# Gate and up projections of the SwiGLU turned round: activation forms as the held operand, 512 weight columns streaming

## The chip, the cores and the metric

The kernel runs on one core of a Trainium2 chip. The metric is the device time of one execution in microseconds (us). The kernel before has a median of 2325.04 us over three runs (2324.38 to 2325.2). The profiled execution shown here took 2325.69 us, of which 2323.9 us is the span from the first instruction to the last.

The engines are called as in the profile: PE is the matrix engine, PEld its weight loads, DVE the vector engine, ACT the scalar engine, POOL the general one and SP the queue that issues most transfers. In a matmul one operand, 128 columns wide, is held in the array (the "weights" of PE) and the other streams past it; the number of streaming columns is the last number of the shape in a row (128x256, 128x512).

## The reference

One layer of a hybrid encoder on 512 tokens with 2048 channels, in float32:

```python
h = rms_norm(x, norm1_g)
p = h @ w_in                      # columns for three mixers
y = concat(rwkv7, rglru, retention)
x = x + y @ w_out
h = rms_norm(x, norm2_g)
x = x + (silu(h @ ffn_w_gate) * (h @ ffn_w_up)) @ ffn_w_down
return rms_norm(x, final_norm_g)
```

The feed-forward width is 5632. The change touches the line with `ffn_w_gate` and `ffn_w_up` (two 2048 x 5632 matrices) and what lies directly beside it.

## The kernel before

Every float32 matmul is done as three: both operands are cut into a high part (rounded to the short format by a cast on ACT) and a low part (the remainder, a subtraction on DVE), and high·high, high·low and low·high are added up in one PSUM bank. `split` makes the two parts of a weight tile, `mm3` issues the three matmuls (lines 161 to 163 of the profile).

The gate and up projections are done with Strassen's scheme (Winograd's variant): the two matrices, each in two halves of channels, are the blocks b11, b21 (gate) and b12, b22 (up); the activations in two halves of channels and two halves of tokens give seven forms f = 0 to 6. Seven products of 1024 channels replace eight. Sums of weight blocks are DVE additions over [128, 1024], sums of results are DVE operations on PSUM banks.

The stages around it, in the order of the program:

1. `w_out`: the output projection. For each of 16 channel tiles PE adds up 16 channel blocks; then x1 = x + that is stored, squared into `acc`, scaled by `norm2_g`, and when both halves are there `make_forms` writes the seven forms, high and low. Five of eight form groups (NFA = 5) have tiles of their own (FAH, FAL); three lie in HH and HL, which hold `w_out`'s own operand, so those wait until that is consumed (the list `late`).
2. `gate_up(ct)` for 44 tiles of 128 feed-forward columns. The weight tile [128 channels, 128 columns] is held, the form [128 channels, 256 tokens] streams. A split weight piece is [128, 1024] and carries all eight channel blocks of one product; there are five places for split pieces (`fslot`, NFS = 5) and ten for raw ones. Results are feature-major: columns on partitions, tokens along the free dimension. The norm factor per token (`rB`, copied over all partitions) multiplies the gate result; ACT computes tanh, DVE two more operations, and the tile, with the up part not yet scaled by the norm, is stored to `hscr[ct]` in DRAM.
3. `down(ci, n)` for ten chunks of four feed-forward tiles, and `down_last` for the eleventh. `load_h` brings the tiles of the next chunk from `hscr`, multiplies by `rB` (the norm factor of the up part) and splits them into GH and GLo.

A scheduler sets the order in which each engine's instructions stand, once, when the program is built; work under `tc.high_priority()` is put ahead of other work that is ready. On the chip each engine then runs its list strictly in that order. Tiles live in pools; when `fa.close()` ends the pool of the gate/up stage, the tiles of the down stage (GH, FT, X1, RW2, ...) take over its memory and wait for its last readers.

Of the kernel before, what the change touches and what calls it, by code (L numbers as in the profile page):

```python
# [30 lines left out]
NFA = 5  # L31
# [7 lines left out]
for _n, _c in PAR:  # L39
# [4 lines left out]
CST = [("ident", 128), ("bd1", 128), ("mask", 128), ("maskr", 128),  # L44
       ("zero", 64), ("mD", 1), ("bd2", 2), ("invf", 1), ("sgn", 1), ("qec", 1), ("hec", 1),
# [6 lines left out]
NCST = _o  # L52

# [43 lines left out]
def hybrid_block(ctx: ExitStack, tc: tile.TileContext, A: dict, out: bass.AP, dbg=None):  # L97
# [32 lines left out]
    def c(name):  # L130
        o, n = CO[name]
        return cst[:, o:o + n]
# [49 lines left out]
    rB = cp.tile([128, T], F32, name="rB")  # L182
# [61 lines left out]
    with tc.high_priority():  # L244
        G.memset(zn, 0.0)
        act(zn[:, 0:1], zn[:, 0:1], AF.Tanh)
        nc.sync.dma_start(out=par, in_=A["par"])
        G.dma_start(out=cst, in_=A["cst"])
# [647 lines left out]

    fa = ExitStack()
    ap_ = fa.enter_context(tc.tile_pool(name="fa", bufs=1))
    RB = [ap_.tile([128, 2048], F32, name=f"RB{i}") for i in range(4)]
    FAH = ap_.tile([128, NFA, 7, 256], F32R, name="FAH")  # L900
    FAL = ap_.tile([128, NFA, 7, 256], F32R, name="FAL")
    XW = ap_.tile([128, 2, 1024], F32R, name="XW")
    EV = ap_.tile([128, 2, 3, 256], F32, name="EV")
    GT = ap_.tile([128, 2, T], F32, name="GT")
    UT = ap_.tile([128, 2, T], F32, name="UT")
    acc = rB
# [31 lines left out]
    def make_forms(j, F):  # L938
# [3 lines left out]
        tt(q[:, 7, :], q[:, 2, :], q[:, 6, :], SUB)  # L942
        hi, lo = form(0, j), form(1, j)
        for d, s_ in ((slice(0, 1), slice(0, 1)), (slice(1, 7), slice(2, 8))):
            S.copy(out=hi[:, d, :], in_=q[:, s_, :])
            tt(lo[:, d, :], q[:, s_, :], hi[:, d, :].bitcast(F32), SUB)

    ring.update(raw2=0, rawl=0, last=0, w2=0, gu=0, ft=0, dn=0, wo=0, rb=0, fs=0, ev=0, h=0)
    ob = {}
    late = []  # L950
    sq = UT
    for n, (ct, q) in enumerate(O_PIECES):
        if n % 2 == 0:
            pcs = wpieces1(A["w_out"][n // 2])
        if q == 0:
            xi = GT[:, nxt("h", 2), :]
# [6 lines left out]
        if q == 3:  # L963
# [9 lines left out]
            F = RB[j % 4]  # L973
            act(F[:, 512 * (ct // 8):512 * (ct // 8) + 512], x1, AF.Copy, scale=p("g2", ct))
            if ct >= 8:
                if j < NFA:
                    make_forms(j, F)
                else:
                    late.append((j, F))
    for j, F in late:  # L980
        make_forms(j, F)

    S.copy(out=rB, in_=head_rsqrt(acc, c("mD"), 1, mmb, eps=NORM_EPS))


    ring["rb"] = 8

    def gate_up(ct):
        b11, b21, b12, b22, x = (rslot(nxt("rb", 10)) for _ in range(5))
        with tc.high_priority():  # L990
            for t_, m, half in ((b11, 0, 0), (b21, 0, 1), (b12, 1, 0), (b22, 1, 1)):
                nc.sync.dma_start(out=t_, in_=A["w_gu"][ct, m, half])
        ps = [bank[nxt("gu", 8)] for _ in range(5)]

        def product(raw, f, b, first):
            wh, wl = fslot(nxt("fs", NFS))
            with tc.high_priority():
                split(raw, wh, wl)
            o = ps[b][:, 0:256]
            for j in range(8):  # L1000
                cs = slice(128 * j, 128 * j + 128)
                mm3(o, wh[:, cs], wl[:, cs], form(0, j)[:, f, :], form(1, j)[:, f, :], first and j == 0, j == 7, skip_group_check=not first)

        e = nxt("ev", 2)
# [327 lines left out]
```

## Time and profile before

| What | Value |
|---|---|
| Median of three runs | 2325.04 us |
| Profiled execution | 2325.69 us |
| Its span | 2323.9 us |
| PE busy | 2283.9 us (98%) |
| PEld busy | 2037.9 us (88%) |
| DVE busy | 1696.6 us (73%) |
| ACT busy | 988.6 us (43%) |
| POOL busy | 21.6 us (1%) |
| Granted PE clock over the span | 0.992 of full speed |
| Moved by DMA | 272.99 MB, mean 117 GB/s |

Matmuls overlap in the array, so the duration in a row (283 ns for 256 columns) is longer than the distance between the starts of two neighbours. What a matmul costs in a dense run is that distance. Granted clock 1.00 is 2.4 GHz and 0.50 is 1.2 GHz; the profile shows no other level, and a number between is a mean over a stretch.

The stages on the clock of the span: mixers up to 760 us, `w_out` to 922.7 us, gate and up to 1816.8 us, down and the last norm to the end.

### The profile page before, as it was taken

How to read it: one execution, taken by the hardware profiler on the slowest of the kernel's cores; microseconds unless marked ns; L12 is line 12 of the kernel's file. 1: busy time of each engine (PE TensorE's matmuls, PEld its weight loads, DVE VectorE, ACT ScalarE, POOL GpSimd, SP SyncE). 2: the span in 40 equal slices, each digit the busy share in tenths (PEclk: the TensorE clock that was granted, in tenths of full speed). 3: DMA queues.
4: the chain of work that ended last, by engine and by line, in shares of the span. 5: the costliest groups of instructions: out<-in, count | busy, mean ns of one | idle time of the engine just before them, and what ended most of it. 6: DMA issues, size and time to landing. Idle time of an engine off the chain costs nothing.

```text
span 2323.9 us, 36949 instructions
## 1 busy us (share of the span) xinstructions
PE 2283.9 (98%) x14529; PEld 2037.9 (88%) x14529; DVE 1696.6 (73%) x2925; ACT 988.6 (43%) x1650; POOL 21.6 (1%) x58
## 2 busy tenths in 40 slices
PE   8999999999999999999999999999999999999998
PEld 7878777778888887999999999999999788878887
DVE  7788699687656555888888888888888466576555
ACT  5563464454235444444444444444444432232234
POOL 0000000000000000000000000000000000000000
PEclk9999999999999999999999999999999999999999
DMA  5324233323323444344333343444332554454332
GB/s 199 102 80 112 75 98 93 107 82 108 106 64 106 153 158 148 131 123 123 117 111 115 118 123 114 123 123 122 111 114 91 159 151 135 132 150 128 117 105 73
DMA packets 131757, 272.99 MB, mean 117 GB/s; under 512 B 37296, under 2 KB 43696, under 8 KB 131456
## 3 DMA queue, kind: packets, MB, share of 16 engines
q1 hardware_dynamic: 120880, 250.47, 36.1%
q10 hardware_dynamic: 8448, 12.59, 1.4%
q0 software_dynamic: 2256, 7.58, 1.0%
q8 instruction: 114, 1.87, 0.3%
q14 instruction: 59, 0.48, 0.1%
HBM read 241.36 MB, written 27.66 MB: 116 GB/s over the span
## 4 chain that ended last, share of the span: by engine, by line
PE 91%; DVE 6%; ACT 1%; issue 1%; DMA 1%; DVEq 0%; SPq 0%; ACTq 0%
PE bank L161 28%; PE bank L162 28%; PE bank L163 28%; PE bank L166 5%; DVE M L140 1%; DVE WL L140 1%; PE bank L569 1%; PE bank L592 1%; DVE M L149 0%; DMA FT<-hscr 0%; DVE M L404 0%; DVE X L140 0%; DVE M L406 0%; DVE SM L140 0%; PE bank L493 0%
## 5 line engine op out<-in xcount | busy, mean ns | idle before, releaser
L161 PE MATMUL bank<-HH,WH 128*128 128x512 f32 (+1 forms) x1297 | 474.6, 366 | 9.1 <-ACT HH L152 6.2
L163 PE MATMUL bank<-HH,WL 128*128 128x512 f32 (+1 forms) x1297 | 472.4, 364 | 0.0
L162 PE MATMUL bank<-HL,WH 128*128 128x512 f32 (+1 forms) x1297 | 472.0, 364 | 0.0
L157 ACT CAST WH<-RAW 128x512 fp32r<-128x512 f32 (+1 forms) x356 | 236.1, 664 | 466.4 <-PE bank L162 403.2
L140 DVE TENSOR_TENSOR WL<-RAW,WH 128x512 fp32r<-128x512 f32 (+1 forms) x356 | 263.4, 740 | 139.8 <-ACT WH L157 137.9
L161 PEld LDWEIGHTS bank<-HH,WH 128*128 128x128 f32 x1297 | 246.1, 190 | 46.5 <-ACT HH L152 6.2
L163 PEld LDWEIGHTS bank<-HH,WL 128*128 128x128 f32 x1297 | 245.9, 190 | 36.3 <-issue 1.4
L162 PEld LDWEIGHTS bank<-HL,WH 128*128 128x128 f32 x1297 | 246.2, 190 | 35.6 <-issue 1.4
L161 PE MATMUL bank<-GH,WH 128*128 128x512 f32 x640 | 250.5, 392 | 6.6 <-ACT WH L157 4.3
L163 PE MATMUL bank<-GH,WL 128*128 128x512 f32 x640 | 250.4, 392 | 0.0
L162 PE MATMUL bank<-GLo,WH 128*128 128x512 f32 x640 | 250.4, 392 | 0.0
L140 DVE TENSOR_TENSOR X<-X,bank 128x512 f32<-128x512 f32 (+1 forms) x178 | 115.6, 655 | 143.0 <-PE bank L163 141.9
L163 PE MATMUL bank<-FAH,WL 128*128 128x256 f32 x615 | 174.8, 284 | 3.0 <-DVE WL L140 3.0
L161 PE MATMUL bank<-FAH,WH 128*128 128x256 f32 x615 | 174.9, 284 | 0.2 <-ACT WH L157 0.2
L162 PE MATMUL bank<-FAL,WH 128*128 128x256 f32 x615 | 174.6, 284 | 0.0
L162 PE MATMUL bank<-FAL,HH 128*128 128x256 f32 x615 | 174.0, 283 | 0.0
L163 PE MATMUL bank<-FAH,HL 128*128 128x256 f32 x615 | 174.0, 283 | 0.0
L161 PE MATMUL bank<-FAH,HH 128*128 128x256 f32 x615 | 173.9, 283 | 0.0
L161 PEld LDWEIGHTS bank<-GH,WH 128*128 128x128 f32 x640 | 121.2, 189 | 32.9 <-ACT WH L157 4.7
L157 ACT CAST HH<-RB 128x1024 fp32r<-128x1024 f32 x90 | 94.4, 1049 | 129.2 <-PE bank L162 79.6
L157 ACT CAST WH<-RB 128x1024 fp32r<-128x1024 f32 x87 | 91.4, 1050 | 126.9 <-PE bank L162 80.2
L163 PEld LDWEIGHTS bank<-GH,WL 128*128 128x128 f32 x640 | 121.1, 189 | 26.1 <-DVE WL L140 0.6
(255 smaller groups left out, 4980.5 us busy)
## 6 DMA issues: line engine op xcount, KB each, us to landing
RB<-in_w_gu_dram SPq DMA_DIRECT2D x132, 512.0 KB, 3.8
RAW<-in_w_in_dram SPq DMA_DIRECT2D x76, 512.0 KB, 3.5
RAW<-in_w_dn_dram SPq DMA_DIRECT2D x96, 256.0 KB, 2.7
RAW<-in_w_gu_dram SPq DMA_DIRECT2D x44, 512.0 KB, 3.7
RW<-in_w_dn_dram SPq DMA_DIRECT2D x80, 256.0 KB, 2.7
RAW<-in_w_out_dram SPq DMA_DIRECT2D x32, 512.0 KB, 3.5
hscr<-UT ACTq DMA_DIRECT2D x44, 256.0 KB, 4.2
FT<-hscr SPq DMA_DIRECT2D x40, 256.0 KB, 3.5
```

The lines of the kernel that those rows point to most:

```text
L140: (eng or V).tensor_tensor(out=o, in0=a, in1=b, op=op)
L157: S.copy(out=hi, in_=raw)
L161: PE.matmul(o, wh, xh, start=first, stop=False, **kw)
L162: PE.matmul(o, wh, xl, start=False, stop=False, **kw)
L163: PE.matmul(o, wl, xh, start=False, stop=last, **kw)
L166: PE.matmul(o, l, r, start=start, stop=stop)
L569: PE.matmul(F[:, q, hv[e]], LS[e][:, ch, :], VS[:, ch, hv[e]], start=(q == 0 and e == 0), stop=True, skip_group_check=(q > 0 or e > 0))
L592: PE.matmul(F[:, q, :], P_[q][1][:, ch, :], ZBq[:, q, :], start=False, stop=True, skip_group_check=True)
```

## The change

- The roles are exchanged in gate and up. A form [128 channels, 128 tokens] is held, and 512 weight columns stream. The stage runs over 11 blocks (NU) of 512 feed-forward columns, each with seven products on two token tiles of 128. One product is four pieces of [128, 1024] (two channel blocks by 512 columns), each used by twelve matmuls.
- Results are token-major, one PSUM bank for each token tile: bA, bB, bC are three pairs of banks, each used by two or three of the seven products. The norm factor is now one number per partition (`rh`, `r2h`), used as the scale of ACT's tanh and as the scalar of a DVE operation; both gate and up get it here, so `load_h` no longer multiplies by `rB`.
- The down stage still wants feature-major tiles, so each block ends with 16 transposes of [128, 128] on PE into two banks (6 and 7), four copies on ACT and four stores.
- Sums of weight blocks are now made once for 512 columns, over [128, 2048].
- Raw blocks: eight tiles of [128, 2048], one for each half block, no second copy. Split pieces: three places instead of five, since NFA is 4, four form groups now lie in HH and HL, and memory is taken by E, H, X2, G1. The late forms are written form by form (the order in which products ask for them) instead of group by group.
- Small things: `cst` is brought in two parts, three tiles move to the mixers' pool, RW2 is allocated earlier in the down pool, and the first chunk's `hscr` tiles go through FT instead of RAW.

The core of the diff:

```diff
-    def rslot(i):
-        return RB[i // 2][:, 1024 * (i % 2):1024 * (i % 2) + 1024] if i < 8 else RAW[:, i - 8, :]
-    NFS = 5
+        if i < 2:
+            return tuple(w[:, 2 * i:2 * i + 2, :].rearrange("p a b -> p (a b)") for w in (WH, WL))
+        return tuple(w.rearrange("p k t -> p (k t)")[:, 7168:8192] for w in (HH, HL))
...
+    for d, s_ in ((0, 0), (1, 2), (4, 5), (3, 4), (5, 6), (2, 3), (6, 7)):
+        for j, F in late:
+            form_put(j, F, slice(d, d + 1), slice(s_, s_ + 1))
-    S.copy(out=rB, in_=head_rsqrt(acc, c("mD"), 1, mmb, eps=NORM_EPS))
+    rq = head_rsqrt_stat(acc, c("mD"), 1, mmb, eps=NORM_EPS)
+    rh, r2h = drv[:, 0:4], drv[:, 4:8]
...
+    blocks = ((RB[0], RB[1]), (RB[4], RB[5]), (RB[2], RB[3]), (RB[6], RAWb))
...
-            wh, wl = fslot(nxt("fs", NFS))
-            with tc.high_priority():
-                split(raw, wh, wl)
-            o = ps[b][:, 0:256]
-            for j in range(8):
-                cs = slice(128 * j, 128 * j + 128)
-                mm3(o, wh[:, cs], wl[:, cs], form(0, j)[:, f, :], form(1, j)[:, f, :], ...)
+            for jj in range(4):
+                wh, wl = fslot(nxt("fs", 3))
+                with tc.high_priority():
+                    split(raw[jj // 2][:, 1024 * (jj % 2):1024 * (jj % 2) + 1024], wh, wl)
+                for t in range(2):
+                    tk = slice(128 * t, 128 * t + 128)
+                    for i in range(2):
+                        j, cs = 2 * jj + i, slice(512 * i, 512 * i + 512)
+                        mm3(bs[t], form(0, j)[:, f, tk], form(1, j)[:, f, tk], wh[:, cs], wl[:, cs], ...)
...
+        product(b11, 0, bA, True)
+        with hp_():
+            for t in two:
+                S.copy(out=E_[:, t, :], in_=bA[t])
+        block(b11, b11, b12)
+        product(b21, 1, bA, False)
+        with hp_():
+            for t in two:
+                act(G_[:, t, :], bA[t], AF.Tanh, scale=rh[:, t:t + 1])
+                stt(G_[:, t, :], G_[:, t, :], 1.0, bA[t], ADD, MUL)
+        block(b12, b12, b22)
+        product(b12, 4, bB, True)
+        product(b11, 3, bC, True)
+        block(b11, b11, b22)
+        product(b11, 5, bA, True)
+        with hp_():
+            for t in two:
+                tt(E_[:, t, :], bA[t], E_[:, t, :], SUB)
+                tt(H_[:, t, :], bB[t], E_[:, t, :], ADD)
+                tt(X_[:, t, :], bC[t], H_[:, t, :], ADD)
+        block(b21, b21, b11)
+        product(b21, 2, bB, True)
+        with hp_():
+            for t in two:
+                tt(H_[:, t, :], bB[t], H_[:, t, :], SUB)
+                act(bB[t], H_[:, t, :], AF.Tanh, scale=rh[:, 2 + t:3 + t])
+                stt(H_[:, t, :], bB[t], 1.0, H_[:, t, :], ADD, MUL)
+                stt(X_[:, t, :], H_[:, t, :], r2h[:, 2 + t:3 + t], X_[:, t, :], MUL, MUL)
+        product(b22, 6, bC, False)
+        with hp_():
+            for t in two:
+                tt(E_[:, t, :], bC[t], E_[:, t, :], ADD)
+                stt(G_[:, t, :], G_[:, t, :], r2h[:, t:t + 1], E_[:, t, :], MUL, MUL)
+            for f in range(4):
+                b = bank[6 + nxt("tr", 2)]
+                for t in range(4):
+                    PE.transpose(b[:, 128 * t:128 * t + 128], (G_, X_)[t // 2][:, t % 2, 128 * f:128 * f + 128], ident)
+                st = H_[:, nxt("st", 2), :]
+                S.copy(out=st, in_=b)
+                S.dma_start(out=hscr[4 * u + f], in_=st)
...
-            f = FT[:, nxt("ft", 4), :] if ci else RAWs[i]
+            f = FT[:, nxt("ft", 4), :]
...
-                tt(f, f, rB, MUL)
```

`product(raw, f, banks, first)` is one product: four pieces, each split and then used by twelve matmuls. `block(o, a, b_)` is the sum of two blocks, two DVE additions over [128, 2048], and stands under high priority.

**Order on DVE where one block follows the other.** First the list of DVE in the kernel before, somewhere in the middle of gate and up. EV, UT, GT and the banks are results of 256 tokens; WL, HL and XW on the left are low parts of split pieces; RB and RAW on the left are sums of weight blocks.

```order
L140 TENSOR_TENSOR EV_6007<-bank0_82,EV_6007 128x256
L140 TENSOR_TENSOR HL_81<-RB3_6003,HH_80 128x1024
L140 TENSOR_TENSOR WL_79<-RAW_77,WH_78 128x1024
L140 TENSOR_TENSOR RAW_77<-RAW_77,RB1_6001 128x1024
L140 TENSOR_TENSOR EV_6007<-bank1_83,EV_6007 128x256
L140 TENSOR_TENSOR XW_6006<-RAW_77,XW_6006 128x1024
L140 TENSOR_TENSOR UT_6009<-bank2_84,EV_6007 128x256
L140 TENSOR_TENSOR WL_79<-RAW_77,WH_78 128x1024
L140 TENSOR_TENSOR RAW_77<-RAW_77 128x1024
L140 TENSOR_TENSOR GT_6008<-bank3_85,EV_6007 128x256
```

Now the list of DVE in the changed kernel, where a block begins: bank4 is the last product's bank of the block that ends; RB0 and RB1 hold b11 of the new one, RB2 and RB3 its b12, RB4 and RB5 its b21.

```order
L141 TENSOR_TENSOR WL_78<-RB0_6002,WH_77 128x1024
L141 TENSOR_TENSOR E_6011<-bank4_85,E_6011 128x512
L141 TENSOR_TENSOR RB0_6002<-RB0_6002,RB2_6004 128x2048
L150 SCALAR_TENSOR_TENSOR G1_6014<-G1_6014,drv_71,E_6011 128x512
L141 TENSOR_TENSOR RB2_6004<-RB2_6004,RB6_6008 128x2048
L141 TENSOR_TENSOR WL_78<-RB1_6003,WH_77 128x1024
L141 TENSOR_TENSOR HL_80<-RB1_6003,HH_79 128x1024
L141 TENSOR_TENSOR WL_78<-RB4_6006,WH_77 128x1024
L141 TENSOR_TENSOR RB1_6003<-RB1_6003,RB3_6005 128x2048
L141 TENSOR_TENSOR WL_78<-RB4_6006,WH_77 128x1024
L141 TENSOR_TENSOR RB3_6005<-RB3_6005,RAW_76 128x2048
L141 TENSOR_TENSOR HL_80<-RB5_6007,HH_79 128x1024
```

Before, a sum of blocks or a result stands between two splits; now all four sums of [128, 2048] that b11 and b12 take part in stand between the second split of the new block and its seventh, with two operations on results among them.

**Order on PE where the fifth product ends and the sixth begins.** bank1 is the second of bA, bank2 the first of bB.

```order
L162 MATMUL bank1_82<-HH_79 128x512
L163 MATMUL bank1_82<-HL_80,HH_79 128x512
L164 MATMUL bank1_82<-HH_79,HL_80 128x512
L162 MATMUL bank2_83<-WH_77,FAH_6009 128x512
L163 MATMUL bank2_83<-WL_78,FAH_6009 128x512
```

The sixth product writes bB directly behind the fifth's last matmul, with nothing between them; DVE reads bB for H_ only after it has read bA for E_.

**Order on ACT where gate and up end.** First before: bank7 holds results of the last tile, GH0 to GH3 are the operand of the down stage's first chunk.

```order
L1015 COPY EV_6007<-bank7_89 128x256
L157 CAST HH_80<-RB3_6003 128x1024
L1023 COPY GT_6008<-bank7_89 128x256
L152 ACTIVATE RB3_6003<-GT_6008 128x512
L1039 DMA hscr_98<-UT_6009 128x512
L157 CAST GH0_16004<-RAW_77 128x512
L157 CAST GH2_16008<-RAW_77 128x512
```

And in the changed kernel, where bank6 and bank7 hold the transposes and H is the tile that is stored:

```order
L158 CAST WH_77<-RAW_76 128x1024
L1058 COPY H_6012<-bank6_87 128x512
L1058 COPY H_6012<-bank7_88 128x512
L1059 DMA hscr_97<-H_6012 128x512 x2
L1058 COPY H_6012<-bank6_87 128x512
L1059 DMA hscr_97<-H_6012 128x512
L1058 COPY H_6012<-bank7_88 128x512
L1059 DMA hscr_97<-H_6012 128x512
L158 CAST WH2_12183<-RAW_76 128x512 x3
L158 CAST GH0_12173<-FT_12181 128x512
L158 CAST GH2_12177<-FT_12181 128x512
```

The casts with which the down stage begins now stand behind four copies of transposes and four stores; H has room for two tiles, so the third copy writes where the first store reads.

## Rows read from the trace of the kernel before

**Rows 1.** Page, busy us, share of the span, instructions.
```profile
PE 2283.9 (98%) x14529; PEld 2037.9 (88%) x14529; DVE 1696.6 (73%) x2925; ACT 988.6 (43%) x1650; POOL 21.6 (1%) x58
```
**Rows 2.** Page, chain that ended last, shares by engine.
```profile
PE 91%; DVE 6%; ACT 1%; issue 1%; DMA 1%; DVEq 0%; SPq 0%; ACTq 0%
```
**Rows 3.** Stretches: length, PE, PEld, DVE, ACT, POOL busy, clock, DMA, GB/s.
```profile
922.70:1816.80 894.10, 890.93 (x7405) 890.07 (x7403) 733.73 (x855) 375.41 (x443) 0.00 (x0) 1.00 0.39 117
1816.80:1826.80 10.00, 5.66 (x15) 4.02 (x14) 8.74 (x15) 6.03 (x11) 0.00 (x0) 0.66 0.54 171
...
1000.00:1080.64 80.64, 80.64 (x674) 80.64 (x674) 66.39 (x76) 34.09 (x42) 0.00 (x0) 1.00 0.40 119
```
**Rows 4.** Timeline of PE in gate/up: start us, us, engine, line, operation.
```profile
1002.10 0.28 PE L161 MATMUL bank<-FAH,XW 128*128 128x256 f32 x1
...
1006.90 0.28 PE L162 MATMUL bank<-HL,WH 128*128 128x256 f32 x1
```
**Rows 5.** Timeline of PE in the down stage.
```profile
2000.04 0.39 PE L162 MATMUL bank<-GLo,WH 128*128 128x512 f32 x1
...
2005.93 0.39 PE L161 MATMUL bank<-GH,WH 128*128 128x512 f32 x1
```
**Rows 6.** Timeline of PE, four transposes and what follows.
```profile
2285.03 0.60 PE L1166 MATMUL bank<-cst,X 128*128 128x128 f32 x4
...
2285.59 0.28 PE L162 MATMUL bank<-GLo,HH 128*128 128x256 f32 x1
```
**Rows 7.** Timeline of DVE, four operations of 1024 without a pause.
```profile
924.48 1.22 DVE L140 TENSOR_TENSOR HL<-RB,HH 128x1024 fp32r<-128x1024 f32 x1
...
929.02 0.68 DVE L140 TENSOR_TENSOR GT<-GT,bank 128x512 f32<-128x512 f32 x1
```
**Rows 8.** Timeline of DVE, operations of 512 without a pause.
```profile
2039.62 0.68 DVE L140 TENSOR_TENSOR X<-X,bank 128x512 f32<-128x512 f32 x1
2040.21 0.68 DVE L140 TENSOR_TENSOR WL<-RAW,WH 128x512 fp32r<-128x512 f32 x1
```
**Rows 9.** Timeline of ACT: a cast of 1024, a copy out of a bank.
```profile
1002.67 1.05 ACT L157 CAST WH<-RAW 128x1024 fp32r<-128x1024 f32 x1 [2.35 <-DVE RAW L140]
...
1827.00 0.58 ACT L1100 COPY X<-bank 128x512 f32<-128x512 f32 x1 [0.62 <-PE bank L163]
```
**Rows 10.** Timeline of PE, its longer waits (idle before, and releaser).
```profile
516.38 0.65 PE L622 MATMUL bank<-cst,M 128*128 128x128 f32 x4 [1.50 <-DVE M L140]
518.24 0.66 PE L622 MATMUL bank<-cst,M 128*128 128x128 f32 x4 [1.21 <-DVE M L149]
602.10 0.47 PE L161 MATMUL bank<-HH,WH 128*128 128x512 f32 x1 [1.67 <-DVE M L140]
929.16 0.58 PE L163 MATMUL bank<-FAH,WL 128*128 128x256 f32 x1 [2.96 <-DVE WL L140]
2058.01 0.47 PE L161 MATMUL bank<-GH,WH 128*128 128x512 f32 x1 [2.28 <-DVE X L140]
```
**Rows 11.** Stretches with and without a fall of the clock.
```profile
517.60:520.80 3.20, 2.02 (x7) 1.52 (x8) 2.38 (x4) 0.17 (x1) 0.00 (x0) 0.80 0.61 191
601.00:604.00 3.00, 1.90 (x8) 1.61 (x9) 2.87 (x7) 0.00 (x0) 0.00 (x0) 1.00 0.17 31
```
**Rows 12.** Timeline of PE where gate/up ends and down begins.
```profile
1816.66 0.28 PE L163 MATMUL bank<-HH,HL 128*128 128x256 f32 x1
...
1821.27 0.80 PE L161 MATMUL bank<-GH,WH 128*128 128x512 f32 x1 [4.34 <-ACT WH L157]
...
1826.76 0.43 PE L161 MATMUL bank<-GH,WH 128*128 128x512 f32 x1
```
**Rows 13.** Page, DMA issues: times, KB each, median us to landing.
```profile
hscr<-UT ACTq DMA_DIRECT2D x44, 256.0 KB, 4.2
FT<-hscr SPq DMA_DIRECT2D x40, 256.0 KB, 3.5
```
**Rows 14.** The lines that touch hscr: ns min/median/max, first and last start.
```profile
L1085 SPq DMA_DIRECT2D RAW<-hscr x4: 320/375/424, 1774.4 to 1783.7; - x4
```

More of the change, by code (lines that the diff above doesn't have):

```diff
@@ L942, in make_forms, with form_put @@
         tt(q[:, 7, :], q[:, 2, :], q[:, 6, :], SUB)
+    def form_put(j, F, d, s_):
+        q = F.rearrange("p (s t) -> p s t", t=256)
         hi, lo = form(0, j), form(1, j)
[L944 to L948, printed above, removed]
+        S.copy(out=hi[:, d, :], in_=q[:, s_, :])
+        tt(lo[:, d, :], q[:, s_, :], hi[:, d, :].bitcast(F32), SUB)
+    ring.update(raw2=0, rawl=0, last=0, w2=0, fs=0, ft=0, dn=0, wo=0, h=0, st=0, tr=0)
     ob = {}
     late = []
-    sq = UT
+    sq = H_
     for n, (ct, q) in enumerate(O_PIECES):
@@ L990, in gate_up @@
+    blocks = ((RB[0], RB[1]), (RB[4], RB[5]), (RB[2], RB[3]), (RB[6], RAWb))
+    def gate_up(u):
+        b11, b21, b12, b22 = blocks
         with tc.high_priority():
             for t_, m, half in ((b11, 0, 0), (b21, 0, 1), (b12, 1, 0), (b22, 1, 1)):
-                nc.sync.dma_start(out=t_, in_=A["w_gu"][ct, m, half])
-        ps = [bank[nxt("gu", 8)] for _ in range(5)]
-        def product(raw, f, b, first):
-            wh, wl = fslot(nxt("fs", NFS))
-            with tc.high_priority():
-                split(raw, wh, wl)
-            o = ps[b][:, 0:256]
-            for j in range(8):
-                cs = slice(128 * j, 128 * j + 128)
-                mm3(o, wh[:, cs], wl[:, cs], form(0, j)[:, f, :], form(1, j)[:, f, :], first and j == 0, j == 7, skip_group_check=not first)
@@ L1004, in gate_up @@
-        e = nxt("ev", 2)
-        e1, u2, u3 = (EV[:, e, i, :] for i in range(3))
-        G_, U_ = GT[:, e, :], UT[:, e, :]
-        t1, t2 = slice(0, 256), slice(256, 512)
-        def hi(o, a, b_, op):
-            with tc.high_priority():
-                tt(o, a, b_, op)
-        product(b11, 0, 0, True)
-        with tc.high_priority():
-            S.copy(out=e1, in_=ps[0][:, 0:256])
-        hi(x, b12, b22, ADD)
-        hi(b12, b11, b12, ADD)
-        hi(b11, b11, x, ADD)
-        product(b11, 5, 1, True)
@@ L1033, in gate_up @@
-        with tc.high_priority():
-            tt(G_, G_, rB, MUL)
-            f = x[:, 0:512]
-            act(f, G_, AF.Tanh, scale=0.5)
-            stt(G_, f, 1.0, G_, ADD, MUL)
-            stt(U_, G_, 0.5, U_, MUL, MUL)
-            S.dma_start(out=hscr[ct], in_=U_)
-    for ct in range(NCT):
-        gate_up(ct)
+                for i in range(2):
+                    nc.sync.dma_start(out=t_[i], in_=A["w_gu"][u, m, half, i])
+        bA, bB, bC = (bank[0], bank[1]), (bank[2], bank[3]), (bank[4], bank[5])
@@ new lines, in product @@
+        def product(raw, f, bs, first):
+            for jj in range(4):
[4 more added lines that the diff above has]
+                    tk = slice(128 * t, 128 * t + 128)
+                    for i in range(2):
+                        j, cs = 2 * jj + i, slice(512 * i, 512 * i + 512)
+                        mm3(bs[t], form(0, j)[:, f, tk], form(1, j)[:, f, tk], wh[:, cs], wl[:, cs],
+                            first and j == 0, j == 7, skip_group_check=not first)
@@ new lines, in block @@
+        def block(o, a, b_):
+            with tc.high_priority():
+                for i in range(2):
+                    tt(o[i], a[i], b_[i], ADD)
+        two = range(2)
+        hp_ = tc.high_priority
+        product(b11, 0, bA, True)
[8 more added lines that the diff above has]
+                stt(G_[:, t, :], G_[:, t, :], 1.0, bA[t], ADD, MUL)
@@ L1043, in hybrid_block @@
+    for u in range(NU):
+        gate_up(u)
     fa.close()
```

71 lines of the change are left out of this document (27 added, 44 removed).

## The prediction

> **What bounds the kernel now.** The first view is the page's busy table: PE is busy for 98% of the span, DVE for 73%, ACT for 43% [rows 1]. The chain that ended last says the same: 91% of it is PE, 6% DVE [rows 2]. So time is won by making PE's stream shorter and lost wherever PE waits. The second view is the table of stretches. Gate and up take 894.1 us at full clock, with PE and its weight loads both busy almost all the time; four tiles, which is what one block of 512 columns will be, take 80.64 us with DVE busy for 66.4 [rows 3]. The third view is the timeline of PE, for the distance of neighbouring starts. In gate and up 40 matmuls of 256 columns lie between the two rows shown: 4.80/40 = 0.1200 us each [rows 4]. The stage has 44 x 7 x 8 x 3 = 7392 of them: 887.0 us. The other 7.1 us of the stage lie at its start, where PE waits 2.96 us for a split [rows 10] and runs slowly behind it. In the down stage 26 matmuls of 512 columns take 5.89 us: 0.2265 each [rows 5].
>
> **The change part by part.**
>
> *Matmuls.* 11 x 7 x 2 x 8 x 3 = 3696 of 512 columns replace 7392 of 256. 3696 x 0.2265 = 837.1, so -49.9 us. At 2.4 GHz 256 columns are 106.7 ns and 512 are 213.3; both rows are 13.3 ns above that, and the change pays this once where two stood. The down stage holds and streams tiles of the same shapes and kinds, so I see no other price; the ends are 0.225 and 0.2275 (-55 to -46).
>
> Here the Trainium skill speaks against the change: "TensorE: Matmul & The Clock Gate", section "Back-to-back issue gap", gives N/2.4 + 2.5 ns for a warm stream. By it the pair would save 2.5 ns, 9 us in all, and the forecast would be 41 us later. The rows show 13.3 ns and not 2.5, and they decide.
>
> *Transposes.* 11 x 16 = 176 new ones on PE. Four transposes and one matmul of 256 took 0.56 us [rows 6]; less 0.12 that is 0.11 each: +19.4 us. None of it is beside other PE work. The ends are 0.09 (16 us) and 0.15, with what the matmul behind them loses (26).
>
> *Wait between fifth and sixth product*, once a block. The sixth writes bB, and H_ must have read bB first, for which E_ must have been taken from bA, which is complete only with the fifth product's last matmul. The order has nothing else for PE there. A result is there 0.39 - 0.23 = 0.16 us after PE could go on [rows 5]; then E_ for the second token tile, 0.60 to the next operation, H_ 0.68 [rows 8], and two handovers of about 0.05 (an estimate): 1.6 us. 11 x 1.6 = +17.6. Queued behind it are DVE's splits for the sixth product, but two pieces are ready by then. The ends are 1.3 (DVE alone) and 2.3 (DVE late by one operation).
>
> *Wait at the beginning of a block.* The split places are three, so at most two pieces are ready ahead of PE, 2 x 12 x 0.2265 = 5.4 us of work. Let T be the end of a block's last matmul. The second piece of the new block goes where the third from last lay, free at T - 2.7; with the lag of 0.16, a cast of 1.05 [rows 9] and a subtraction of 1.22 [rows 7] it is ready at T - 0.3. From there DVE's list up to the seventh split holds two results (0.60 each), four sums over [128, 2048] and five splits. A split costs (929.02 - 924.48)/4 = 1.135 [rows 7]. A sum of 2048 isn't in the trace: 512 cost 0.60, 1024 cost 1.135, so 0.535 for 512 more, 2.2 in all (at least 4 x 0.535 = 2.1, at most two single ones, 2.44). Sum: 1.2 + 8.8 + 5.7 = 15.7, so the seventh piece's low part is there at T + 15.5. PE's list has, ahead of the matmul that needs it, four whole pieces (10.9), the first token tile's half of the next two (2.7), one matmul and two transposes (0.4): T + 14.0. PE waits 1.5 us. Behind it stand E_ and G_ of the second token tile, on which 14 transposes wait (0.1 to 0.2), and these need banks 6 and 7 emptied by ACT twice, at 0.58 a copy [rows 9], with two matmuls to cover it (0.3 to 0.5). Together 2.1 us at ten boundaries: +21. The ends are 0 (no sum late) and 3.9 (sums at 2.44, results at 0.68).
>
> *DVE and ACT in all.* DVE has a block of 28 x 1.135 + 8 x 2.2 + 18 x 0.62 = 60.5 us to do, ACT 28 x 1.05 + 10 x 0.6 = 35. Both fit in 80, so only bunching costs; the removed `rB` copy and its transposes are under 1 us.
>
> *Start of the stage.* 7.1 us went there before. Now four form groups come late, but in the order in which products ask for them. b12's second half is loaded only when the last group, in the same tile, is written; its sum then stands ahead of the third split of the third product. I put this wait and the slow clock behind it at 6 us: -1.1, with 0 to 15 as ends, since both kernels take this from the same operations.
>
> *End of the stage.* Before, the first matmul of down came 1821.27 - 1816.78 = 4.5 us after the last of gate/up, and at 1826.76 PE was back at its pace [rows 12]: 10.0 us with 12 matmuls in them. Its operand had been fetched from `hscr` 35 us earlier [rows 14]. Now ACT's list has the four copies and stores ahead of GH0's cast. The last G_ is ready at T + 1.6, the first copy ends at 2.7, its store is issued at 3.3 and lands 4.2 later [rows 13]; the third copy has to wait for that: 7.5. Third and fourth copy and their stores bring it to 8.8, three casts of WH2, GH0, GH2 and the first WH (0.62 each) to 12.5. So 8 us are added. Then h1 and h3 are fetched behind loads that wait for these very splits: some 16 + 3.5 [rows 13], PE waits again, and is in step at T + 20 with 12 matmuls done: 10.0 worse, of which 1.8 are transposes already counted: +8.2. The ends are 2 (the stores land in 2) and 16.
>
> *Down.* 44 multiplications leave DVE, 26 us. Nothing on PE's path but the wait of 2.28 behind a DVE bunch [rows 10]: -2.3 (0 to -5).
>
> *Sum.* -49.9 + 19.4 + 17.6 + 21 - 1.1 + 8.2 - 2.3 = +12.9 us. The profiled execution took 2325.69, its span 2323.9 and 1.8 around it, which stay: 2338.6. The median is 0.65 below the profiled execution, so **2338 us**.
>
> **The rivals.**
>
> *Cover holds (faster).* The waits at the beginning of a block don't come, because DVE enters it ahead: 66 of 80 us busy before without one wait of PE [rows 3, 10] speaks for it, three places instead of five against it. 2338 - 21 = 2317; with half the wait before the sixth product as well, 2308. It decides if the seventh split ends before T + 14.
>
> *About level.* Half of the waits: 2338 - 11 = 2327.
>
> *The clock falls in each block (slower still).* Waits of 1.50 and 1.21 with transposes between them brought the clock to 0.80 [rows 10, 11]; a lone wait of 1.67 left it at 1.00 [rows 10, 11]. At a block's beginning a wait of 1.5 is followed within 4 us by 14 transposes with waits among them. A fall costs between 0.2 x 3.2 = 0.6 us [rows 11] and 0.34 x 10 = 3.4 us [rows 3]; at 1.7, ten times, 2338 + 17 = 2355.
>
> *DVE is the bound.* Sums at 2.44 and results without overlap: 1.8 us more a block, 2358.
>
> **How the numbers follow.** Forecast 0.48 (its own range 2330 to 2350), clock 0.17, DVE bound 0.05, level 0.15, cover 0.15. All but the last two are slower by more than 0.2%, about what a measurement of this kernel can tell from no change (4.7 us, so 2320.4 to 2329.7 is the same): slower 0.70, same 0.15, faster 0.15. The range reaches from 2316, which leaves out the lower part of the cover case, to 2362, which leaves out a clock that falls at the high price.
>
> **What would show it.** Right: starts 0.2265 apart in gate and up; a block of about 81.8 us against 80.64; in each block a wait of about 1.6 us of PE for H on DVE, and one or two of together 1.5 us for a WL or HL early in the block; 176 transposes at 0.11; the first matmul with GH some 12 us after the last of gate/up. Wrong: starts further apart than 0.2275, a block below 80 us, a clock below 1.00 in the middle of the stage, a wait of PE for ACT copies or for a DMA of raw blocks, which I price at nothing because a tile's loads are issued a third of a block or more ahead.

## The result and the profile after

The changed kernel takes 2342.03 us (median of four runs, 2336.34 to 2344.16) beside 2325.12 for the kernel before (2324.38 to 2325.25): a ratio of 1.007, 95% interval 1.005 to 1.009. It is slower, 4 us above the 2338 foretold and well inside the range.

The page's busy line and its line of the chain, and a line of its DMA part:

```profile
PE 2270.9 (97%) x11005; PEld 1859.6 (79%) x11005; DVE 1627.8 (69%) x2661; ACT 1000.3 (43%) x1646; POOL 22.0 (1%) x59
...
PE 82%; DVE 11%; issue 4%; ACT 2%; DMA 1%; SPq 0%; ACTq 0%; DVEq 0%
...
hscr<-H ACTq DMA_DIRECT2D x44, 256.0 KB, 2.2
```

PE is busy for 13 us less than in [rows 1] and yet the span is 18.4 us longer. In the chain DVE has gone from 6% [rows 2] to 11%: PE now waits where it did not. The stretches tell in which stage (columns as in [rows 3]: the stage of gate and up, one block of 512 columns, the passage to down, the rest):

```profile
925.58:1826.95 901.37, 871.86 (x3865) 707.13 (x3863) 688.73 (x619) 384.92 (x421) 0.00 (x0) 1.00 0.33 112
1000.00:1081.79 81.79, 79.19 (x354) 64.25 (x353) 62.23 (x55) 35.04 (x39) 0.00 (x0) 1.00 0.34 116
1826.95:1851.50 24.55, 12.51 (x40) 8.29 (x40) 10.00 (x16) 10.16 (x19) 0.00 (x0) 0.72 0.67 232
1851.50:2342.30 490.80, 479.77 (x2249) 402.61 (x2247) 271.24 (x463) 161.25 (x288) 0.53 (x1) 0.99 0.41 124
```

The stage takes 7.3 us more than in [rows 3], at a mean clock of 1.00, and PE stands idle for 30 us of it. (The mean hides 3.4 us at half clock in the first block; see "Start of the stage" below.) From first transpose to first transpose a block has a length of 81.79 to 81.81 us nine times running (81.8 was foretold). The passage takes 24.55 us, with 22 matmuls of down in it. The groups of PE's waits within the stage (waited for: us in total, times, longest us):

```profile
PE bank L162 <- DVE H L141: 17.3, 11, 1.6
PE bank L163 <- DVE WL L141: 7.8, 15, 0.7
PE bank L163 <- DVE HL L141: 3.1, 6, 0.7
PE bank L162 <- ACT WH L158: 1.3, 1, 1.3
```

The first is the wait before the sixth product; the next two are those at the beginning of a block, one of them (0.53 us) and the fourth in the middle of the first block. On the timeline of PE, the first kind in the first block and the second kind at the beginning of the second block:

```profile
987.14 0.47 PE L162 MATMUL bank<-HH,FAH 128*128 128x512 f32 x1 [1.57 <-DVE H L141]
987.45 0.40 PE L163 MATMUL bank<-HL,FAH 128*128 128x512 f32 x1
...
1015.64 0.50 PE L163 MATMUL bank<-WL,HH 128*128 128x512 f32 x1 [0.32 <-DVE WL L141]
1024.59 0.50 PE L163 MATMUL bank<-WL,HH 128*128 128x512 f32 x1 [0.71 <-DVE WL L141]
```

A wait costs more than its idle time. The matmul ahead of 987.14 began at 987.14 - 1.57 - 0.39 = 985.18, and 987.45 is two matmuls on: 2.27 us where 2 x 0.2265 would do, 1.82 lost for an idle time of 1.57. And on DVE at the beginning of the next block:

```profile
1091.09 2.28 DVE L141 TENSOR_TENSOR RB<-RB,RB 128x2048 f32<-128x2048 f32 x1
1093.29 0.75 DVE L150 SCALAR_TENSOR_TENSOR G<-G,drv,E 128x512 f32<-128x512 f32 x1
1093.95 2.28 DVE L141 TENSOR_TENSOR RB<-RB,RB 128x2048 f32<-128x2048 f32 x1
1096.16 1.22 DVE L141 TENSOR_TENSOR WL<-RB,WH 128x1024 fp32r<-128x1024 f32 x1
```

A sum over 2048 is followed 2.20 us later, as the forecast had it. The end of the stage on PE, where [rows 12] answer, and on ACT:

```profile
1826.72 0.39 PE L164 MATMUL bank<-WH,HL 128*128 128x512 f32 x1
...
1837.32 1.31 PE L162 MATMUL bank<-GH,WH 128*128 128x512 f32 x2 [6.23 <-ACT WH L158]
...
1845.89 0.80 PE L162 MATMUL bank<-GH,WH 128*128 128x512 f32 x1 [4.29 <-ACT WH L158]
```
```profile
1829.30 1.07 ACT L1058 COPY H<-bank 128x512 f32<-128x512 f32 x2 [9.19 <-PE bank L1056]
...
1832.02 0.59 ACT L1058 COPY H<-bank 128x512 f32<-128x512 f32 x1 [1.65 <-DMA hscr<-H]
...
1834.05 1.66 ACT L158 CAST WH<-RAW 128x512 fp32r<-128x512 f32 x3 [0.40 <-ACT H L1058]
1835.61 1.13 ACT L158 CAST GH<-FT 128x512 fp32r<-128x512 f32 x2
```

The third copy waits for the store that reads its place; behind it stand the casts of down's first operands. PE waits 6.23 us, starts at half clock, and waits again, 4.29 us.

One part of the 18.4 us is not the change's. The stage begins 2.9 us later than in [rows 3], behind mixers whose work the change leaves as it is. The stretch from 625 to 665 us of four kernels, in this order: before, after, and the fifth and the eighth kernel below, which are alike up to here.

```profile
625.00:665.00 40.00, 37.77 (x336) 33.55 (x334) 16.72 (x40) 12.26 (x38) 0.47 (x1) 0.83 0.15 38
```
```profile
625.00:665.00 40.00, 37.85 (x311) 33.21 (x310) 14.90 (x35) 11.00 (x34) 0.00 (x0) 0.74 0.11 24
```
```profile
625.00:665.00 40.00, 37.85 (x310) 33.14 (x308) 14.92 (x35) 10.60 (x33) 0.00 (x0) 0.74 0.11 25
```
```profile
625.00:665.00 40.00, 37.77 (x338) 33.77 (x338) 16.93 (x42) 12.32 (x39) 1.06 (x2) 0.83 0.17 41
```

The granted clock (the third number from the right) is on average 0.83 or 0.74 over the same 40 us: 13.7 or 20.5 us at half clock. Of the profiled executions, those with the shorter fall (before, and experiments 1, 2, 6, 7 and 8) start the stage at 921.4 to 923.3 us, those with the longer one (the changed kernel, and experiments 3, 4 and 5) at 925.6 to 926.5. That enters every median below, and is why the experiments are read by stage as well.

### The profile page after: what moved, and what is told of

It is laid out like the page before. It is cut to its first block, busy times and chain, and to the rows that moved or that the text cites. A ratio compares the mean times of both kernels' runs of the same rounds, so it can differ in the third digit from the quotient of the medians.

```text
span 2342.3 us, 29241 instructions
## 1 busy us (share of the span) xinstructions
PE 2270.9 (97%) x11005; PEld 1859.6 (79%) x11005; DVE 1627.8 (69%) x2661; ACT 1000.3 (43%) x1646; POOL 22.0 (1%) x59
## 4 chain that ended last, share of the span: by engine, by line
PE 82%; DVE 11%; issue 4%; ACT 2%; DMA 1%; SPq 0%; ACTq 0%; DVEq 0%
PE bank L163 25%; PE bank L162 25%; PE bank L164 25%; PE bank L167 5%; DVE WL L141 3%; DVE RB L141 2%; DVE M L141 1%; ACT WH L158 1%; PE bank L573 1%; DVE E L141 1%; DVE HL L141 1%; PE bank L1056 1%; PE bank L596 1%; DVE M L150 0%; ACT HH L158 0%
## 5 line engine op out<-in xcount | busy, mean ns | idle before, releaser
L162 PE MATMUL bank<-HH,WH 128*128 128x512 f32 x928 | 370.5, 399 | 8.8 <-ACT HH L153 5.8
L164 PE MATMUL bank<-HH,WL 128*128 128x512 f32 x928 | 368.3, 397 | 0.0
L163 PE MATMUL bank<-HL,WH 128*128 128x512 f32 x928 | 367.8, 396 | 0.0
L141 DVE TENSOR_TENSOR WL<-RB,WH 128x1024 fp32r<-128x1024 f32 x191 | 232.3, 1221 | 131.4 <-ACT WH L158 130.8
L162 PE MATMUL bank<-GH,WH 128*128 128x512 f32 x640 | 251.0, 393 | 10.5 <-ACT WH L158 10.5
L163 PE MATMUL bank<-WL,HH 128*128 128x512 f32 (+1 forms) x604 | 219.1, 363 | 7.8 <-DVE WL L141 7.8
L162 PE MATMUL bank<-WH,HH 128*128 128x512 f32 (+1 forms) x604 | 215.9, 360 | 1.3 <-ACT WH L158 1.3
L164 PE MATMUL bank<-WH,HL 128*128 128x512 f32 (+1 forms) x604 | 216.8, 359 | 0.0
L162 PE MATMUL bank<-WH,FAH 128*128 128x512 f32 x412 | 162.2, 394 | 11.0 <-DVE H L141 11.0
L163 PE MATMUL bank<-WL,FAH 128*128 128x512 f32 x412 | 160.5, 390 | 0.0
L164 PE MATMUL bank<-WH,FAL 128*128 128x512 f32 x412 | 160.5, 391 | 0.0
```

Of the source, the lines that this page charges most:

```text
L141: (eng or V).tensor_tensor(out=o, in0=a, in1=b, op=op)
L162: PE.matmul(o, wh, xh, start=first, stop=False, **kw)
L163: PE.matmul(o, wh, xl, start=False, stop=False, **kw)
L164: PE.matmul(o, wl, xh, start=False, stop=last, **kw)
```

## The experiments

The theory was the sum of the prediction: PE's stream became shorter by the fixed part of 3696 matmuls, and that is given away to transposes, to a bank that has to be read first, to DVE's list at the beginning of a block, and to ACT's list at the end. Rivals are named in each expectation. Every kernel ran in five rounds beside the kernel before; medians are compared with 2325.35 (23 runs) for the first four and 2325.91 (9 runs) for the others.

**1. Another bank for the sixth product** (`e1_banks67`)

```diff
-        bA, bB, bC = (bank[0], bank[1]), (bank[2], bank[3]), (bank[4], bank[5])
+        bA, bB, bC, bD = (bank[0], bank[1]), (bank[2], bank[3]), (bank[4], bank[5]), (bank[6], bank[7])
...
-        product(b21, 2, bB, True)
+        product(b21, 2, bD, True)
         with hp_():
             for t in two:
-                tt(H_[:, t, :], bB[t], H_[:, t, :], SUB)
-                act(bB[t], H_[:, t, :], AF.Tanh, scale=rh[:, 2 + t:3 + t])
-                stt(H_[:, t, :], bB[t], 1.0, H_[:, t, :], ADD, MUL)
+                tt(H_[:, t, :], bD[t], H_[:, t, :], SUB)
+                act(bD[t], H_[:, t, :], AF.Tanh, scale=rh[:, 2 + t:3 + t])
+                stt(H_[:, t, :], bD[t], 1.0, H_[:, t, :], ADD, MUL)
```

> Against the changed kernel at 2342.0 us. The sixth product of a block writes banks 6 and 7 instead of banks 2 and 3, so its first matmul no longer has to wait until H_ has read bank 2. Theory (a dependence through the bank, 1.57 us in each of 11 blocks): the wait for H goes and nothing takes its place, since the first pieces of the sixth product lie ready; 11 x 1.57 = 17.3 us less, a block of 80.2 instead of 81.79, about 2325 us. Rival (DVE is late there anyway): the wait turns up at the next piece or at the seventh product, 2335 us or more.

Measured: 2319.41 us (11 runs), ratio to before 0.9974 (0.9964 to 0.9984). The groups of PE's waits within the stage, where H is no longer among them:

```profile
PE bank L163 <- DVE WL L141: 7.7, 15, 0.7
PE bank L163 <- DVE HL L141: 3.1, 6, 0.7
```

A block, as a stretch:

```profile
1000.00:1079.96 79.96, 78.95 (x354) 64.32 (x353) 62.15 (x54) 35.04 (x39) 0.00 (x0) 1.00 0.35 119
```

The waits for WL and HL are what they were, so nothing took the place of the one removed. 81.79 - 79.96 = 1.83 us a block, which is the 1.82 read from the rows above and not the idle 1.57. The stage is 21.95 us shorter (879.42 against 901.37), and the median 22.6 where 17.3 were expected: eleven times 1.83 are 20.1, and 1.8 more lie in the first block, where the clock did not fall in this execution. The theory holds; the rival, a late DVE, falls. One bank pair turns the change from slower into faster.

**2. Two sums of a block done later** (`e2_sums_later`)

```diff
+    one = ap_.tile([128, 1], F32, name="one")
...
-        block(b12, b12, b22)
+        with hp_():
+            ts(one, E_[:, 1, 0:1], 0.0, MUL, 1.0, ADD)
+            for i in two:
+                stt(b12[i], b22[i], one, b12[i], MUL, ADD)
```

> Against the changed kernel at 2342.0 us. The two sums b12 + b22 of a block (2.28 us each on DVE) are made to wait for the result of the block's first product through a factor of 1.0, so they leave the list that DVE has to do at the beginning of a block. Theory (DVE's list ahead of the seventh split is what PE waits for there): PE's waits for WL and HL at the beginning of a block, 1.03 us by the rows, go, and with them the wait of the transposes for G; 1.0 to 1.5 us in each of ten blocks, about 2329 us (2326 to 2332). Rival (three split places hold the pieces back whatever DVE does between): within 2 us of 2342. Second rival (the sums are then late for the third product): a new wait of up to 2 us for a WL there, 2342 or more.

Measured: 2319.35 us (7 runs), ratio 0.9973 (0.9962 to 0.9984). What is left of PE's waits in the stage behind its first block:

```profile
PE bank L162 <- DVE H L141: 17.3, 11, 1.6
```

A block, as a stretch:

```profile
1000.00:1079.97 79.97, 78.40 (x354) 64.38 (x353) 62.32 (x56) 35.08 (x38) 0.00 (x0) 1.00 0.35 119
```

The waits for WL and HL are gone, and 1.82 us a block with them: the cause is DVE's list and not the number of split places, which is still three. The gain is more than the 1.0 to 1.5 expected, and the median is below the expected 2326 to 2332. Two waits seen as 1.03 us cost about 1.6, since each also loses 0.16, by which a matmul's 0.39 exceeds its 0.2265, and 0.11 at the next start, which comes 0.34 later. The remaining 0.2 lay in the transposes, which stand behind the late G. Their weight loads wait for it in the ten later blocks, first in the changed kernel, then here (L1056 and L1060 are the same line of code):

```profile
PEld bank L1056 <- DVE G L150: 5.6, 20, 0.4
PEld bank L1060 <- DVE G L150: 3.5, 19, 0.2
```

The stage has become 22.3 us shorter (879.05 against 901.37): 18.2 in ten blocks and 4.1 in the first, where the same sums had stood ahead of splits. That part I had not expected. Some 1.7 of the 4.1 is a fall of the clock that did not come here.

**3. No transposes** (`e3_no_transposes`)

```diff
-                b = bank[6 + nxt("tr", 2)]
-                for t in range(4):
-                    PE.transpose(b[:, 128 * t:128 * t + 128], (G_, X_)[t // 2][:, t % 2, 128 * f:128 * f + 128], ident)
                 st = H_[:, nxt("st", 2), :]
-                S.copy(out=st, in_=b)
+                for t in range(4):
+                    S.copy(out=st[:, 128 * t:128 * t + 128], in_=(G_, X_)[t // 2][:, t % 2, 128 * f:128 * f + 128])
```

> Against the changed kernel at 2342.0 us. The 176 transposes are left out; ACT copies the untransposed 128 x 128 parts into the store places, so the values in hscr are not the transposed ones. Theory (0.11 us each, none beside other PE work, and 0.2 to 0.5 us of waiting around them in a block): 19.4 + 3 = 22 us less, about 2320 us. Rival (PE would stand at the beginning of a block for its late splits anyway, so the transposes partly fill a wait): 8 to 12 us less, 2330 to 2334. Second rival (each also delays the matmul behind it, 0.15 us): 26 us and more, 2315.

Measured: 2332.10 us (8 runs), ratio 1.0026 (1.0015 to 1.0037): 10 us below the changed kernel, the size of the first rival. The waits of its stage tell that this is no price of a transpose:

```profile
PE bank L163 <- DVE WL L141: 10.1, 15, 0.7
PE bank L162 <- ACT E L1023: 5.7, 10, 0.6
PE bank L163 <- DVE HL L141: 4.4, 6, 0.9
```

PE comes sooner to splits that are no earlier, and waits 3.6 us more for them; and a new wait for ACT's copy E_ out of the first product's bank has come, ten times, because ACT's list now has four small copies for one, behind G. Both take back what the transposes gave. So the rival has some truth (they did lie partly in time in which DVE was late), but the run does not separate a transpose from its surroundings; the sixth does.

**4. The end of the stage** (`e4_end`)

```diff
-                st = H_[:, nxt("st", 2), :]
+                st = (E_ if u == NU - 1 and f > 1 else H_)[:, nxt("st", 2), :]
...
-            f = FT[:, nxt("ft", 4), :]
+            f = FT[:, nxt("ft", 4), :] if ci else RAWs[i]
```

> Against the changed kernel at 2342.0 us. At the last block the four parts of the SwiGLU result have four store places instead of two, and the first four tiles that down loads go into RAW (as in the kernel before) instead of FT, which puts all four loads ahead of the loads of down's later weights on SP's queue. Theory (at the end of gate/up PE waits 6.2 us for a chain on ACT that holds a wait of 1.65 us for a store, and 4.3 us for tiles loaded behind weights): the first matmul of down comes 2 us earlier, the second wait goes, about 6 us less, 2336 us. Rival (down's first weight loads now come later and PE waits for them instead): within 2 us of 2342.

Measured: 2330.42 us (8 runs), ratio 1.0028 (1.0017 to 1.0038). The stage, as a stretch, is as long as in the changed kernel:

```profile
926.19:1827.76 901.57, 872.12 (x3865) 707.00 (x3863) 688.95 (x619) 385.38 (x421) 0.00 (x0) 1.00 0.33 112
```

Behind it, on the timeline of PE, there is one long wait instead of two:

```profile
1835.87 0.79 PE L162 MATMUL bank<-GH,WH 128*128 128x512 f32 x1 [3.99 <-ACT WH L158]
...
1842.04 0.39 PE L164 MATMUL bank<-GH,WL 128*128 128x512 f32 x1
```

The first matmul of down comes 8.1 us after the stage's last instead of 10.4, the 4.29 is gone, and 6.2 us later PE is at its pace. From the stage's last matmul to the end of the program it is 2334.8 - 1827.76 = 507.0 us against 2342.3 - 1826.95 = 515.4: 8.3 less, where 6 was expected. The medians differ by 11.6. What the rest is, the runs do not show; the slowest run of this kernel (2336.57, the profiled one) is 7.6 below the slowest of the changed kernel (2344.16), which is near the 8.3. The two halves of the edit were not run apart.

**5. The three edits together** (`e5_three_edits`)

The diffs of 1, 2 and 4.

> The edits of the first, second and fourth experiment together. Theory (three separate losses: 1.57 us of idle time and some 0.16 of restart before the sixth product, 1.8 us at a block's beginning, some 8 us at the end of the stage): from the second experiment's 2319.4 us another 11 x 1.73 = 19 and 8 come off, about 2292 us, a block of 78.2 us. Rival (DVE, which now has 60 us to do in 78, is late somewhere else once PE no longer waits): above 2300 us, with new waits for WL or HL.

Measured: 2293.38 us (4 runs), ratio to before 0.9855 (0.9838 to 0.9872): 48.7 us below the changed kernel and 32.5 below the one before. The stage, what follows it, and a block:

```profile
925.98:1785.23 859.25, 859.21 (x3865) 708.26 (x3863) 688.61 (x630) 385.84 (x421) 0.00 (x0) 1.00 0.34 118
1785.23:2291.50 506.27, 489.51 (x2287) 409.23 (x2286) 280.83 (x479) 170.72 (x305) 0.53 (x1) 0.99 0.42 132
1000.00:1078.17 78.17, 78.17 (x354) 64.47 (x353) 62.24 (x56) 35.13 (x38) 0.00 (x0) 1.00 0.35 121
```

PE is busy for all but 0.04 us of the stage. The block closes: 336 x 0.2265 = 76.10 for matmuls and 2.07 for 16 transposes and all else; with 1.83 for the bank and 1.82 for the sums that is 81.82, the changed kernel's 81.79. The losses were separate, and DVE with 62 us of work in 78 is not late anywhere else; the rival falls.

**6. Every transpose twice** (`e6_transposes_twice`, on the fifth)

```diff
-                for t in range(4):
+                for t in (0, 0, 1, 1, 2, 2, 3, 3):
                     PE.transpose(b[:, 128 * t:128 * t + 128], (G_, X_)[t // 2][:, t % 2, 128 * f:128 * f + 128], ident)
```

> The fifth kernel with every one of the 176 transposes done twice into the same place (the second writes the same values). Theory (0.11 us each and nothing beside them): 176 x 0.11 = 19.4 us more than the fifth kernel. Rival (a part of them fills time in which PE would wait): 8 to 12 us more. Second rival (each also delays the matmul behind it): 26 us more.

Measured: 2311.25 us (5 runs), ratio to before 0.9934 (0.9917 to 0.9950); 17.9 above the fifth. A block:

```profile
1000.00:1080.00 80.00, 79.98 (x370) 66.31 (x369) 62.25 (x56) 35.34 (x39) 0.00 (x0) 1.00 0.35 119
```

Sixteen more take 80.00 - 78.17 = 1.83 us, 0.114 each, and nothing hides them where PE does not wait for anything else. That is the price that the third run couldn't give, and 176 of them make 20.1 us. The median shows 17.9, since this kernel's profiled execution starts the stage 3.8 us earlier than the fifth's; its stage is 20.0 longer, of which 1.6 lie in one block where PE once waits 1.35 us for ACT.

**7. Matmuls of 256 columns in the new arrangement** (`e7_256_columns`, on the fifth)

```diff
-                    for i in range(2):
-                        j, cs = 2 * jj + i, slice(512 * i, 512 * i + 512)
-                        mm3(bs[t], form(0, j)[:, f, tk], form(1, j)[:, f, tk], wh[:, cs], wl[:, cs],
-                            first and j == 0, j == 7, skip_group_check=not first)
+                    for i in range(4):
+                        j, cs, o = 2 * jj + i // 2, slice(256 * i, 256 * i + 256), slice(256 * (i % 2), 256 * (i % 2) + 256)
+                        mm3(bs[t][:, o], form(0, j)[:, f, tk], form(1, j)[:, f, tk], wh[:, cs], wl[:, cs],
+                            first and j == 0, j == 7, skip_group_check=True)
```

The two halves of a bank are begun and summed apart here, and the sums are not the reference's; number, shape and order of the instructions are what the run is read for.

> The fifth kernel with each gate/up matmul cut in two of 256 moving columns, with the same held operand and the two halves of the same bank: 7392 matmuls instead of 3696, everything else as it is. Theory (what the change saved is the fixed 13.3 ns of each matmul, 0.1200 us for 256 columns against 0.2265 for 512): 7392 x 0.1200 - 3696 x 0.2265 = 49.9 us more than the fifth kernel. Rival (the saving came from what is held and what moves, or from the scale and the products' order, not from the number of matmuls): under 10 us more.

Measured: 2342.97 us (5 runs), ratio to before 1.0073 (1.0059 to 1.0088); 49.6 above the fifth, where 49.9 was expected. By the stage it is 51.9 more (911.19 against 859.25), so that the medians agree to 0.3 us is in part luck. The stage as a stretch:

```profile
923.27:1834.46 911.19, 911.19 (x7561) 905.89 (x7559) 691.81 (x630) 383.38 (x421) 0.00 (x0) 1.00 0.32 112
```

And on the timeline of PE two starts that lie 43 matmuls apart:

```profile
1000.06 0.28 PE L164 MATMUL bank<-HH,HL 128*128 128x256 f32 x1
...
1005.22 0.28 PE L162 MATMUL bank<-WH,FAH 128*128 128x256 f32 x1
```

5.16/43 = 0.1200 us, the distance of [rows 4] with the roles of the operands exchanged. What is held and what moves is worth nothing that shows here; the number of matmuls, each with its own weight load, is worth 50 us. A matmul's part and its load's part in that were not taken apart.

**8. The multiplications of down put back** (`e8_down_multiplies`, on the fifth)

```diff
                 nc.sync.dma_start(out=f, in_=hscr[ct])
+                tt(f, f, f, MAX)
                 split(f, GH[slot], GLo[slot])
```

> The fifth kernel with one DVE operation more for each of the 44 tiles that down loads (the tile's maximum with itself, in place of the multiplication by rB that the change took away there). Theory (down became faster because these left DVE's list): 2 to 4 us more than the fifth kernel, among it a wait of PE of about 2 us in one place. Rival (the down stage differs for another reason): within 1 us of the fifth kernel.

Measured: 2291.36 us (4 runs), ratio to before 0.9855 (0.9838 to 0.9872). By the medians it is 2 us below the fifth, and the expectation would have missed; but its profiled execution had the better mixers (stage from 921.54, fifth 925.98), and four runs do not average that out. The stretch from the stage's end on:

```profile
1780.80:2289.30 508.50, 490.82 (x2287) 410.00 (x2286) 303.11 (x519) 171.14 (x305) 0.54 (x1) 0.99 0.42 131
```

And its one wait on the timeline of PE in down:

```profile
2025.09 0.47 PE L162 MATMUL bank<-GH,WH 128*128 128x512 f32 x1 [1.56 <-DVE X L141]
```

508.50 against 506.27: 2.2 us more, and a wait for X is back; in the down stage of the fifth kernel there is none. Not all of the 2.2 is its price, for the clock differs at the beginning of this stretch, first in the fifth kernel and then here:

```profile
1785.23:1801.23 16.00, 10.17 (x43) 7.49 (x43) 9.13 (x15) 9.79 (x19) 0.00 (x0) 0.89 0.73 243
1780.80:1796.80 16.00, 10.49 (x39) 7.62 (x39) 11.21 (x19) 9.85 (x18) 0.00 (x0) 0.79 0.73 238
```

By the starts on ACT's list this execution is 0.7 us later than the fifth's before that wait and 2.5 us later after it, so the wait costs 1.8 us. That the operations bring the wait is shown; its price is just under the 2 to 4 us of the theory, and the medians cannot decide 2 us.

## Why the prediction was right, and where its terms were off

The account of the profiled span, which grew from 2323.9 to 2342.3 us, by the prediction's steps (us):

| step | foretold | measured | from |
|---|---|---|---|
| fewer matmuls | -49.9 | -49.9 | the two pitches; run 7: 49.6 by the median, 51.9 by its stage |
| transposes | +19.4 | +20.1 | run 6: 0.114 x 176 |
| wait before the sixth product | +17.6 | +20.1 | run 1: 11 x 1.83 |
| beginning of a block | +21 | +18.2 | run 2: 10 x 1.82 |
| start of the stage, and the rest of it | -1.1 | +0.6 | stage 901.4 less the four above |
| end of the stage | +8.2 | +10.5 | passage 24.55, less 22 matmuls, less the same of [rows 12], less 16 transposes |
| down | -2.3 | -4.1 | 490.8 against 497.1, with 10 matmuls fewer left |
| mixers | 0 | +2.9 | not the change: clock 0.74 or 0.83 over the same 40 us |
| sum | +12.9 | +18.4 | |

Each term but the first is off by 0.7 to 2.9 us, with either sign. That the sum is no more than 5.5 off owes something to luck; that each step came in its place does not.

*Matmuls.* Right in size and cause. The pitch in the changed kernel is 0.2265, the one that down showed [rows 5]. The Trainium skill, "TensorE: Matmul & The Clock Gate", section "Back-to-back issue gap", has 2.5 ns beside the columns for a matmul by itself, which the prediction weighed for the stream; by that, run 7 would have come out 9 us above the fifth kernel. It came out 49.6 above, and 13.3 ns stand for these matmuls. The sustained spacing that the same section gives for 512 columns, about 131 ns, is not met here either: 226.5.

*Transposes.* Right: 0.114 where 0.11 was read from [rows 6].

*Wait before the sixth product.* Right in place and releaser, 2.5 us short in all. The foretold 1.6 was the whole loss: 0.16 until the last result is there and about 1.4 for the two operations and the handovers. Measured are 0.16, an idle time of 1.57, and 0.08 because the first matmul after the wait is followed 0.31 us later and not 0.2265: PE loses 1.82 each time.

*Beginning of a block.* The mechanism was right: DVE's list ahead of the late splits, with sums of 2.2, and the transposes behind G. The late split ends where it was foretold: PE's second wait is over 15.6 us after the first block's end (1024.59 less 1009.00, where the next block's first matmul starts), foretold 15.5. The size was 0.3 us a block too high, and that lies in the transposes: the two waits for splits cost 1.6 with what follows them, where 1.5 was foretold, and the transposes' waits about 0.2, where 0.6 was. The second run returned all of it.

*Start of the stage.* Put at 6 us, measured 7.7 (7.1 as before, and 0.6). The wait came in the third product of the first block, on a split, and the slow clock behind it, as foretold (two waits on the timeline, and a stretch around them):

```profile
955.65 0.73 PE L162 MATMUL bank<-WH,HH 128*128 128x512 f32 x2 [1.32 <-ACT WH L158]
956.91 0.78 PE L163 MATMUL bank<-WL,HH 128*128 128x512 f32 x1 [0.53 <-DVE WL L141]
...
955.00:962.00 7.00, 5.83 (x17) 4.39 (x18) 3.56 (x4) 3.39 (x4) 0.00 (x0) 0.76 0.44 142
```

A mean of 0.76 over 7 us is 3.4 us at half clock, which costs some 1.7. The second run took the waits and the fall away, 4.1 us in all, so the forecast had not missed these sums of the first block.

*End of the stage.* The chain was right link by link: copies, the store that holds the third copy, casts, and tiles loaded behind weights. Two links were off against each other. The stores land in 2.2 us and not in the 4.2 of [rows 13], so the first matmul comes 10.4 us after the stage's last and not 12.5. The second wait ends 18.9 us after it, near the foretold 19.5, but behind it 13 matmuls run at half clock (0.43 apart), which I had put at nothing: PE is at its pace 24.5 us after the stage's last matmul and not 20. The fourth run removed 8.3 us of it.

*Down.* The wait of 2.28 went [rows 10]; I took away its idle time alone. On the trace of before the clock fell behind it: a stretch from 2056 to 2064 us has a granted clock of 0.79, and eight matmuls start 0.43 apart there.

```profile
2056.00:2064.00 8.00, 5.99 (x19) 4.81 (x20) 6.59 (x12) 1.35 (x3) 0.00 (x0) 0.79 0.47 141
```

2.28 and 0.24 of restart and some 1.6 at half clock make the 4.1. In the eighth run the same wait came back as 1.56, at a clock of 1.00, and 1.8 us with it. The operations that the change took out of down are the cause of the wait; how much it costs hangs on whether the clock falls.

*The rivals.* The cover did not hold, and DVE was not the bound (62 us in 78 in the fifth kernel without one wait). From the second block on the clock did not fall, though PE waits 1.57 us in each block and 0.3 and 0.7 us ahead of transposes; so the rival that gave the clock a fall in each block (0.17) falls. What kind of work stands around a wait does not explain it. In the first block the clock fell behind 1.32 and 0.53 us, and in the kernel before behind 2.28 us, all among full matmuls; it held behind 1.15 and 0.53 us in the first block of experiment 1, and behind 1.56 us in experiment 8. Why it falls behind one wait and not behind another, the runs don't show.

## What to carry to other kernels

Count what a matmul costs beside its columns from the distance of starts of both widths in one trace, multiply by the number saved, and then spend as much care on the waits that the new order makes: here the transposes and the waits took all of 50 us and more, and a spare bank pair, two sums done a product later, and store places and loads arranged anew at the end got 49 back. A wait of PE for a bank or a split costs its idle time plus about a quarter of a microsecond, each time round the loop. And read an experiment by the stage it edits, and the clock in short stretches: untouched stages moved the times by up to 5 us, more than some of these edits did, and a mean clock of 1.00 over 900 us hid a fall of 3.4 us.

## What the runs showed of the hardware

- The same mixer instructions ran with a granted clock of 0.74 or 0.83 over 40 us, in the fifth and the eighth kernel, which are alike up to there; around its fall PE waits in both three times 0.46 us for ACT and once 0.76 for DVE, among matmuls of 32 to 128 columns. Of the 4.4 us by which the fifth starts the stage later, 3.3 arise there, and 1.2 in the first 80 us of the span, where the clock is at 1.00.
- A wait of 1.57 us costs PE 1.82 us, and its removal returned 1.83.
- 0.1200 and 0.2265 us for 256 and 512 moving columns hold with weights held or moving.
- Stores of 256 KB to `hscr` landed in 2.2 us from one arrangement and in 4.2 from the other [rows 13], with the same bytes in each; the runs don't show why.
